# The order of sixteen products in a half block: high and low parts in turn, or eight and eight

## The chip, the cores and the metric

The kernel runs on one core of a Trainium2 chip. Its engines work in parallel, each on its own list of instructions in order: TensorE (PE, matrix products; its weight loads are listed as PEld), VectorE (DVE), ScalarE (ACT), GpSimd (POOL) and SyncE (SP, which here only issues DMAs). The metric is the device time of one execution in microseconds; the profile shows one execution, instruction by instruction.

## The reference

One encoder block works on 256 tokens of 2048 channels, all in float32. In short:

```python
proj = h @ w_in[l]                                   # 2048 -> q, k, v, r, af, ab, u (6144), gates (4096)
y_gla = _gla_branch(q, k, v, r, af, ab, ...)         # gated linear attention, both directions
y_hy = _hyena_branch(hy_u, ...)                      # short convolution, then two long ones by FFT
merged = g[:, :, 0, :] * (y_gla @ w_gla_o[l]) + g[:, :, 1, :] * (y_hy @ w_hy_o[l])
h = _layernorm(DEEPNORM_ALPHA * h + merged @ w_out[l], ln1_g[l], ln1_b[l])
ff = jnp.square(jax.nn.relu(h @ w_ff1[l])) @ w_ff2[l]  # 2048 -> 8192 -> 2048
h = _layernorm(DEEPNORM_ALPHA * h + ff, ln2_g[l], ln2_b[l])
```

Nearly all of the arithmetic is in the large products with the weight matrices.

## The kernel before, in words

**Three products for one.** The large products are made in the type float32r. A float32 weight w is split into a high part (whi, rounded to float32r by ACT, line 81) and a low part (wlo = w - whi, by DVE, line 82); the activations are split in the same way and lie side by side, high and low. The kernel adds up high x high, high x low and low x high.

**Weight blocks.** The weights come from device memory as blocks of 128 x 2048 float32 (1 MB each), in the order of their use. `fetch` (line 89) issues the DMA of a block on SP's queue into a tile `raw` (3 buffers) and splits it in two halves of 1024 columns, each with a tile `whi` and a tile `wlo` (3 buffers each). A half therefore holds eight 128 x 128 weight tiles, one for each of eight slices `kt` of the 2048 input channels. `next_block` (line 129) fetches one block more and hands out the oldest, so that two blocks are on their way while one is in use.

**Two ways to use a block.** In a channel pair (`channel_pair`, line 133) the weights are the stationary operand and the activations move. It makes 256 output channels for all 256 tokens, from two blocks, and for each block it takes an accumulator of 512 columns in PSUM: columns 0 to 255 collect high x high and low x high, columns 256 to 511 collect high x low. For each `kt` there are two products: line 143, weight high part, which streams 512 columns (activation high and low), and line 144, weight low part, which streams 256 columns (activation high) and adds into the first 256 columns of the accumulator. So a block takes 32 products, 16 in each half. Behind them ACT copies the second half of the accumulator (line 146) and DVE adds the first half to it (line 147). The channel pairs make q, k, the gates g1 and g2, the hyena inputs (uv, ux, uz), the output projections go and ho, and the first MLP product f (four quarters f0 to f3 of eight pairs each): 96 pairs, 192 blocks, 384 halves. A first block for the gate ranks (pa, lines 370 to 374) has the same loop. In a token group (`token_group`, line 166) the activations are stationary and the weights move, always 512 columns wide (lines 162 to 164): r, v, wo and the second MLP product w. The last column group of wo and of w (lines 790 to 792) is 256 wide.

**One special case.** The first block of f0 runs with `by_tile`: it makes the products for the first 128 tokens, then for the second 128, so that it can begin while the second half of the layer norm is still under way (the transposes ht, line 826).

**Side work.** Between blocks `pump` (line 116) adds smaller jobs that were put off with `later`: the hyena filters (ha, hb, Ca, Sa, Cb, Sb), the gates, scores and outputs of the four attention heads (z, s, o, yt), and the hyena's transforms (Zp, yp, vt, x1t, yT). They use PSUM buffers of their own.

**What sets the order.** The program is written in the order above, and an automatic scheduler then orders the instructions of every engine by a time line that it simulates; where the side work falls between the products is its decision. On the chip every engine follows its list and waits on semaphores.

The lines that the change and the prediction touch: 81 and 82 (split), 96 (DMA of a block), 143 and 144 (channel pair products), 146 and 147 (their sum), 162 to 164 (token groups), 346 (filters, DVE), 373 and 374 (first block), 541 (yt), 675 and 716 (hyena output to device memory and back), 776 and 826 (layer norm and transposes).

Of the kernel before, what the change touches and what calls it, by code (L numbers as in the profile page):

```python
# [16 lines left out]
P = 128  # L17
# [3 lines left out]
KT = D // P  # L21
# [19 lines left out]
def block_kernel(  # L41
# [24 lines left out]
    MM = nc.tensor.matmul  # L66
# [7 lines left out]
    def psum_main(name):  # L74
        return mmp.tile([P, 512], F32, tag="mm", name=name)
# [40 lines left out]
    def pump():  # L116
        clock[0] += 1
        due = sorted((e for e in side if e[0] <= clock[0]), key=lambda e: e[:2])
        for e in due:
            side.remove(e)  # L120
        for e in due:
            e[2]()
# [6 lines left out]
    def next_block():  # L129
        fetch()  # L130
        return queue.popleft()

    def channel_pair(act, name, dst=None, scale=1.0, by_tile=False):
        if dst is None:
            dst = base.tile([P, 2, L], F32, tag="sum", name=f"{name}_s")
        for c in range(2):
            ps = psum_main(f"{name}_{c}").rearrange("p (a b) -> p a b", a=2)
            parts = next_block()
            for ts in ((slice(0, P), slice(P, L)) if by_tile and c == 0 else (slice(0, L),)):
                for kt in range(KT):  # L140
                    hi, lo = parts[kt // 8]
                    js = slice(kt % 8 * P, (kt % 8 + 1) * P)
                    MM(ps[:, :, ts], hi[:, js], act[:, kt, :, ts], start=(kt == 0), stop=False)  # L143
                    MM(ps[:, 0, ts], lo[:, js], act[:, kt, 0, ts], start=False, stop=(kt == KT - 1))  # L144
            low = base.tile([P, L], F32, tag="low", name=f"{name}_l{c}")
            nc.scalar.activation(low, ps[:, 1], AF.Copy, scale=scale)
            nc.vector.scalar_tensor_tensor(dst[:, c], ps[:, 0], scale, low, op0=ALU.mult, op1=ALU.add)
            pump()
        return dst
# [40 lines left out]
    def act_tile(pool, tag, name):  # L190
        return pool.tile([P, KT, 2, L], F32R, tag=tag, name=name)
# [12 lines left out]
    xT = act_tile(base, "xT", "xT")  # L204
# [162 lines left out]
    pa = psum_main("pa").rearrange("p (a b) -> p a b", a=2)  # L367
    fetch()
    parts = next_block()
    for kt in range(KT):  # L370
        hi, lo = parts[kt // 8]
        js = slice(kt % 8 * P, (kt % 8 + 1) * P)
        MM(pa, hi[:, js], xT[:, kt], start=(kt == 0), stop=False)
        MM(pa[:, 0], lo[:, js], xT[:, kt, 0], start=False, stop=(kt == KT - 1))
    nc.scalar.copy(a_low, pa[:, 1])
    nc.vector.tensor_tensor(a_sum[:, 0], pa[:, 0], a_low, op=ALU.add)
    nc.scalar.copy(as_sb, a_sum[:, 0])
# [5 lines left out]
    for dst, nm, sc in ((q_sb, "q", 1.0 / 16.0), (k_sb, "k", 1.0)):  # L383
        for c2 in range(4):
            channel_pair(xT, f"{nm}{c2}", dst[:, 2 * c2:2 * c2 + 2, :], sc)
# [182 lines left out]
    for c2 in range(8):  # L568
        channel_pair(xT, f"g1_{c2}", m_pair(c2))
# [111 lines left out]
    def gla_o_pair():  # L681
        c2 = go_done[0]
        go_done[0] += 1
        ps = channel_pair(yT, f"go{c2}")
        mp = m_pair(c2)
        nc.vector.tensor_tensor(mp, mp, ps, op=ALU.mult)

    go_after = [0, 0, 1, 1, 1, 1, 1, 3]
    for c in range(NCH):
        ps = channel_pair(xT, f"uv{c}")  # L690
# [4 lines left out]
        ps = channel_pair(xT, f"ux{c}")  # L695
# [5 lines left out]
        ps = channel_pair(xT, f"uz{c}")  # L701
# [7 lines left out]
    for c2 in range(8):  # L709
        ps = channel_pair(xT, f"g2_{c2}")  # L710
# [8 lines left out]
    for c2 in range(8):  # L719
        ps = channel_pair(yhT, f"ho{c2}")  # L720
# [22 lines left out]
    def resident(slots):  # L743
        parts = []
        for hi, lo in slots:
            n = fetched[0]
            fetched[0] = n + 1
            raw = wp.tile([P, D], F32, tag="raw", bufs=3, name=f"raw{n}")
            nc.sync.dma_start(raw, wblk[n])
            for h in range(2):  # L750
                cs = slice(h * 1024, (h + 1) * 1024)
                split_hi_lo(hi[:, cs], lo[:, cs], raw[:, cs])
            parts.append([(hi[:, 0:1024], lo[:, 0:1024]), (hi[:, 1024:], lo[:, 1024:])])
        return parts

    def halves(pool, tag, name):
        t = pool.tile([P, 4, D], F32R, tag=tag, name=name)
        return [(t[:, 0], t[:, 1]), (t[:, 2], t[:, 3])]
# [49 lines left out]
    parts = resident([x0] + halves(ep, "f", "wr1"))  # L808
# [67 lines left out]
    parts = resident(halves(ep, "f", "wr2") + halves(ep, "hT", "wr3"))  # L876
# [137 lines left out]
```

## Time and profile before

| | |
|---|---|
| median of 3 runs | 1891.8 us (1891.52 to 1891.81) |
| profiled execution, its own time | 1891.83 us |
| its span | 1890.0 us |
| granted TensorE clock, mean | 0.994 |
| PE busy | 1860.4 us, 10060 matmuls |
| weight loads (PEld) busy | 1599.7 us |
| DVE busy | 1313.6 us |
| ACT busy | 949.5 us |
| read from device memory | 356.66 MB |

A busy time adds up the stretches in which an engine had an instruction under way. Matmuls are pipelined, so that the duration of one is longer than its share of the stream; the distance from one start to the next is what a matmul costs in a stream. In a row of the timeline the columns are the start and the duration in us, the engine, the line, the operation, output and inputs, the sizes of the stationary tile and of the moving one, and the number of instructions. "L144 ... 128x256" streams 256 columns.

### The profile page before, as it was taken

To read this page: it belongs to the slowest core of one execution; us is meant where nothing else is said; L and a number is where in the kernel's file an instruction comes from. 1 tells how busy PE (TensorE), PEld (TensorE's weight loads), DVE (VectorE), ACT (ScalarE), POOL (GpSimd) and SP (SyncE) were. 2 spreads that over 40 slices of the span, in tenths; PEclk is the share of its full clock that TensorE was granted. 3 is DMA by queue.
4 is the path that set the end of the run, shared out by engine and by line. 5 is a ranking of instruction groups with operands and counts; after the bars stand their busy time and mean duration, and the time that the engine had idled before them with its cause. 6 is when DMAs were issued, how large, how long until landed. Compare 5 with 4: busy or idle time off the path is not lost.

```text
span 1890.0 us, 25333 instructions
## 1 busy us (share of the span) xinstructions
PE 1860.4 (98%) x10060; PEld 1599.7 (85%) x10060; DVE 1313.6 (70%) x1702; ACT 949.5 (50%) x1286; POOL 38.3 (2%) x60
## 2 busy tenths in 40 slices
PE   8999999999999999999999998999999999999996
PEld 7887888888888888888888888888888888888886
DVE  6787968875789888888556567666555555555556
ACT  5555556674555555555544444444434443444343
POOL 0000000000000000000000001000000000000001
PEclk9999999999999999999999999999999999999998
DMA  7667764445555555565655764555555555545552
GB/s 289 231 225 251 265 228 161 140 142 204 195 195 199 199 194 189 197 223 191 212 197 183 285 216 153 188 193 186 196 186 198 180 199 187 192 180 199 191 189 110
DMA packets 60583, 375.09 MB, mean 198 GB/s; under 512 B 7216, under 2 KB 10928, under 8 KB 20912
## 3 DMA queue, kind: packets, MB, share of 16 engines
q1 hardware_dynamic: 46512, 324.03, 47.4%
q0 software_dynamic: 5888, 29.36, 4.2%
q10 hardware_dynamic: 8064, 20.07, 3.0%
q8 instruction: 79, 1.29, 0.3%
q14 instruction: 40, 0.33, 0.0%
HBM read 356.66 MB, written 16.78 MB: 198 GB/s over the span
## 4 chain that ended last, share of the span: by engine, by line
PE 93%; DVE 4%; ACT 1%; DMA 1%; issue 1%; ACTq 0%; DVEq 0%; SPq 0%
PE f L143 13%; PE f L144 6%; PE g L143 6%; PE w L163 6%; PE w L164 6%; PE w L162 6%; PE go L143 3%; PE ux L143 3%; PE uz L143 3%; PE uv L143 3%; PE g L144 3%; PE ho L143 3%; PE ho L144 2%; PE uv L144 2%; PE ux L144 2%; PE go L144 2%
## 5 line engine op out<-in xcount | busy, mean ns | idle before, releaser
L82 DVE TENSOR_TENSOR wlo<-raw,whi 128x1024 fp32r<-128x1024 f32 x596 | 728.3, 1223 | 488.2 <-ACT whi L81 487.3
L81 ACT CAST whi<-raw 128x1024 fp32r<-128x1024 f32 x596 | 627.0, 1053 | 772.6 <-PE w L164 186.8
L143 PE MATMUL f<-hT,whi 128*128 128x512 f32 (+1 forms) x1040 | 361.7, 394 | 0.0
L144 PE MATMUL f<-hT,wlo 128*128 128x256 f32 (+1 forms) x1040 | 290.0, 279 | 0.0
L143 PEld LDWEIGHTS f<-hT,whi 128*128 128x128 f32 x1040 | 195.6, 188 | 44.3
L144 PEld LDWEIGHTS f<-hT,wlo 128*128 128x128 f32 x1040 | 197.1, 190 | 0.1
L163 PE MATMUL w<-wlo,f 128*128 128x512 f32 x480 | 186.8, 389 | 0.0
L164 PE MATMUL w<-whi,f 128*128 128x512 f32 x480 | 186.8, 389 | 0.0
L143 PE MATMUL g<-xT,whi 128*128 128x512 f32 x512 | 178.6, 393 | 0.0
L162 PE MATMUL w<-whi,f 128*128 128x512 f32 x480 | 168.0, 389 | 0.0
L144 PE MATMUL g<-xT,wlo 128*128 128x256 f32 x512 | 143.5, 281 | 0.0
L143 PEld LDWEIGHTS g<-xT,whi 128*128 128x128 f32 x512 | 95.7, 187 | 21.1
L162 PEld LDWEIGHTS w<-whi,f 128*128 128x128 f32 x480 | 90.0, 188 | 18.8
L164 PEld LDWEIGHTS w<-whi,f 128*128 128x128 f32 x480 | 90.1, 188 | 18.7
L163 PEld LDWEIGHTS w<-wlo,f 128*128 128x128 f32 x480 | 90.1, 188 | 18.5
L144 PEld LDWEIGHTS g<-xT,wlo 128*128 128x128 f32 x512 | 96.7, 189 | 0.5 <-DVE wlo L82 0.2
L143 PE MATMUL uz<-xT,whi 128*128 128x512 f32 x256 | 91.9, 398 | 0.0
L143 PE MATMUL ux<-xT,whi 128*128 128x512 f32 x256 | 91.7, 398 | 0.0
L143 PE MATMUL go<-yg,whi 128*128 128x512 f32 x256 | 91.1, 397 | 0.0
L143 PE MATMUL uv<-xT,whi 128*128 128x512 f32 x256 | 90.5, 395 | 0.0
L143 PE MATMUL ho<-yh,whi 128*128 128x512 f32 x256 | 88.8, 391 | 0.0
L144 PE MATMUL ux<-xT,wlo 128*128 128x256 f32 x256 | 72.0, 281 | 0.0
(329 smaller groups left out, 3336.7 us busy)
## 6 DMA issues: line engine op xcount, KB each, us to landing
raw<-wblk SPq DMA_DIRECT2D x303, 1024.0 KB, 4.8
Td<-T POOLq DMA_DIRECT2D x16, 768.0 KB, 4.1
Tl<-Td POOLq DMA_DIRECT2D x16, 768.0 KB, 4.5
w<-w4s ACTq DMA_DIRECT2D x16, 512.0 KB, 4.6
zr<-ln_rows ACTq DMA_DIRECT2D x4, 1024.0 KB, 10.9
raw<-wblk SPq DMA_DIRECT2D x4, 512.0 KB, 6.7
xr<-xt SPq DMA_DIRECT2D x4, 512.0 KB, 6.5
dec<-decay_in ACTq DMA_DIRECT2D x8, 256.0 KB, 3.1
```

Of the source, the lines that this page charges most:

```text
L81: nc.scalar.copy(hi, src)
L82: nc.vector.tensor_tensor(lo, src, hi.bitcast(F32), op=ALU.subtract)
L143: MM(ps[:, :, ts], hi[:, js], act[:, kt, :, ts], start=(kt == 0), stop=False)
L144: MM(ps[:, 0, ts], lo[:, js], act[:, kt, 0, ts], start=False, stop=(kt == KT - 1))
L162: MM(pss[tb], sh, wh, start=(kt == 0), stop=False)
L163: MM(pss[tb], sh, wl, start=False, stop=False)
L164: MM(pss[tb], sl, wh, start=False, stop=(kt == KT - 1))
```

## The change

In each half block the products with `kt` from 0 to 7 (or 8 to 15) were issued in turn: high, low, high, low. Now the eight products on the high part come first and the eight on the low part behind them. The same happens in the loop of the first block (pa). Number, operands and results of the products are the same; only their order differs, and the first product of a block still starts the accumulator and its last one still ends it. The scheduler orders the rest anew.

```diff
             ps = psum_main(f"{name}_{c}").rearrange("p (a b) -> p a b", a=2)
             parts = next_block()
             for ts in ((slice(0, P), slice(P, L)) if by_tile and c == 0 else (slice(0, L),)):
-                for kt in range(KT):
-                    hi, lo = parts[kt // 8]
-                    js = slice(kt % 8 * P, (kt % 8 + 1) * P)
-                    MM(ps[:, :, ts], hi[:, js], act[:, kt, :, ts], start=(kt == 0), stop=False)
-                    MM(ps[:, 0, ts], lo[:, js], act[:, kt, 0, ts], start=False, stop=(kt == KT - 1))
+                for h in range(2):
+                    hi, lo = parts[h]
+                    kts = [(kt, slice(kt % 8 * P, (kt % 8 + 1) * P)) for kt in range(8 * h, 8 * h + 8)]
+                    for kt, js in kts:
+                        MM(ps[:, :, ts], hi[:, js], act[:, kt, :, ts], start=(kt == 0), stop=False)
+                    for kt, js in kts:
+                        MM(ps[:, 0, ts], lo[:, js], act[:, kt, 0, ts], start=False, stop=(kt == KT - 1))
...
     parts = next_block()
-    for kt in range(KT):
-        hi, lo = parts[kt // 8]
-        js = slice(kt % 8 * P, (kt % 8 + 1) * P)
-        MM(pa, hi[:, js], xT[:, kt], start=(kt == 0), stop=False)
-        MM(pa[:, 0], lo[:, js], xT[:, kt, 0], start=False, stop=(kt == KT - 1))
+    for h in range(2):
+        hi, lo = parts[h]
+        kts = [(kt, slice(kt % 8 * P, (kt % 8 + 1) * P)) for kt in range(8 * h, 8 * h + 8)]
+        for kt, js in kts:
+            MM(pa, hi[:, js], xT[:, kt], start=(kt == 0), stop=False)
+        for kt, js in kts:
+            MM(pa[:, 0], lo[:, js], xT[:, kt, 0], start=False, stop=(kt == KT - 1))
```

## The prediction

> **What bounds the kernel now.** I read the page first: the busy times and the chain of work that ended last.
>
> ```profile
> span 1890.0 us, 25333 instructions
> PE 1860.4 (98%) x10060; PEld 1599.7 (85%) x10060; DVE 1313.6 (70%) x1702; ACT 949.5 (50%) x1286; POOL 38.3 (2%) x60
> PE 93%; DVE 4%; ACT 1%; DMA 1%; issue 1%; ACTq 0%; DVEq 0%; SPq 0%
> L143 PE MATMUL f<-hT,whi 128*128 128x512 f32 (+1 forms) x1040 | 361.7, 394 | 0.0
> L144 PE MATMUL f<-hT,wlo 128*128 128x256 f32 (+1 forms) x1040 | 290.0, 279 | 0.0
> ```
>
> PE sets the time: it is busy 98% of the span and carries 93% of the chain. The two lines that the change reorders (L143 the high part, 512 columns; L144 the low part, 256 columns) show no idle time before them. Their means (394 and 279 ns) are latencies of overlapping matmuls, so I priced them by the distance from one start to the next, in the timeline of PE. Next, who PE waits for:
>
> ```profile
> PE ht L826 <- DVE zr L776: 5.3, 3, 3.0
> PE pa L373 <- DVE xT L82: 3.9, 1, 3.9
> PE v L163 <- DVE wlo L82: 1.4, 2, 0.9
> PE yt L541 <- DVE y L534: 1.3, 1, 1.3
> PE Cb L226 <- DVE T L346: 0.7, 1, 0.7
> PE v L163 <- DVE rq_t L184: 0.7, 1, 0.7
> ```
>
> Columns: total us, times, longest. None of these is a product of a channel pair waiting for a weight half, so giving wlo more time buys nothing there. What is left is the rate at which PE streams. A stretch of ho:
>
> ```profile
> 1000.16 0.39 PE L143 MATMUL ho<-yh,whi 128*128 128x512 f32 x1
> 1000.39 0.28 PE L144 MATMUL ho<-yh,wlo 128*128 128x256 f32 x1
> 1000.51 0.39 PE L143 MATMUL ho<-yh,whi 128*128 128x512 f32 x1
> ...
> 1004.32 0.39 PE L143 MATMUL ho<-yh,whi 128*128 128x512 f32 x1
> ```
>
> Twelve pairs in 4.16 us: 346.7 ns a pair, 230 ns after the 512-wide and 117 ns after the 256-wide one. The same code in the third quarter of f is slower:
>
> ```profile
> 1500.26 0.40 PE L143 MATMUL f<-hT,whi 128*128 128x512 f32 x1
> 1500.61 0.40 PE L143 MATMUL f<-hT,whi 128*128 128x512 f32 x1
> ...
> 1501.32 0.40 PE L143 MATMUL f<-hT,whi 128*128 128x512 f32 x1
> ```
>
> Three pairs in 1.06 us: 353.3 ns a pair, and it stays so for all of f2 and f3, with no wait in it. So the alternating stream has two rates, and a stretch keeps the one that it has. Streams of one width:
>
> ```profile
> 1844.90 0.40 PE L163 MATMUL w<-wlo,f 128*128 128x512 f32 x1
> ...
> 1846.06 0.39 PE L163 MATMUL w<-wlo,f 128*128 128x512 f32 x1
> ```
> ```profile
> 1853.38 0.39 PE L164 MATMUL w<-whi,f 128*128 128x512 f32 x1
> 1853.61 0.28 PE L790 MATMUL w<-wr,f 128*128 128x256 f32 x1
> 1853.72 0.28 PE L791 MATMUL w<-wr,f 128*128 128x256 f32 x1
> 1853.84 0.28 PE L792 MATMUL w<-wr,f 128*128 128x256 f32 x1
> ```
>
> Long runs of 512-wide matmuls settle at 226.7 ns, long runs of 256-wide ones at 120 ns, each with its own weight load. The first fence stands just behind two 256-wide matmuls: its five steps take 1.16 us where settled ones take 1.133. The second is the other switch.
>
> **The change, part by part.**
>
> *The rate of a settled half.* Instruction counts and operands stay; 192 blocks of channel pairs (and pa) have two halves each, 384 halves in all. Before, eight fast pairs: 8 x 346.7 = 2773 ns. After, from the settled rows: 8 x 226.7 + 8 x 120 = 2773 ns. No gain and no loss: only the two phase effects below are left.
>
> *The slow phase goes.* I took the distance from start to start of every matmul of a channel pair and subtracted the settled price (226.7 or 120 ns), leaving out single steps over 40 ns, which are waits and transposes. The remainder is 3.2 us in f, 3.9 us in uv, ux, uz and go together, 0.8 us in q and k, 0.6 us in g, 0.0 in ho: 8.5 us. f alone checks it: 512 pairs of f2 and f3 by 6.6 ns are 3.4 us. Runs of one width leave that phase: behind the slow f2, the first 512-wide steps of w are 233, 236, 228, 232, 231 and then 227 ns. After five matmuls it has settled, and the new groups are eight long. So -8.5 us.
>
> *Switching costs come in.* From settled 512 to 256 the steps are 114, 119, then 120 ns: 7 ns gained (second fence). From 256 to 512 the first five steps are 3 to 9 ns too long; the cases of the trace sum to 25 to 28 ns, and the last 256-wide step ahead of them is 1 to 3 ns short. Net 15 to 19 ns for a half, and I take 17.5: 384 x 17.5 ns = +6.7 us (5.8 to 7.3). Bounds: nothing, if the groups settle at once as in the alternating rows, up to 384 x 28 = 10.8 us if the 7 ns are not won.
>
> *Side work between the products.* 124 times in the trace a channel pair's product is followed by a matmul of another kind. Where that lands inside a group it starts another settling, up to 20 ns each: 0 to 2.5 us, taken as half, +1.2.
>
> *Weight halves and buffers.* whi is released seven short matmuls (0.84 us) earlier in each half, wlo at the same place, and the first wlo of a half is needed 7 x 0.227 = 1.6 us later. The cast L81 can start earlier and DVE's L82 waits less for it, but PE does not wait for either in these stages. The copy L146 waits, as before, for the block's last low product, so nothing is freed earlier in PSUM. Price 0; the cover is the two blocks fetched ahead.
>
> *The start.* pa's fifth high product comes 4 x 0.21 us (half clock) sooner than now, at about 12.1 us; its xT group is finished at 11.67. The ninth comes at 15.55 as today (its group: 14.5), the thirteenth at 16.5, and the last group is done at 15.77. No wait; 0.
>
> *Order elsewhere.* The order of the changed kernel shows the groups as written, SP's queue unmoved, and on POOL one load of yr put ahead of one store of yd. yr and the split of yh end at 917 us and ho begins at 976, so 59 us cover it. What does move is side work: counted in PE work, the filter products stand 4 to 9 us later in k and r, the first gates 5 us and later heads' scores 2.7 us later in v, the hyena steps 2 to 3 us later. Queued behind a late side product on PE is the main stream, so each is a possible wait; equally, inputs that now come 0.7 to 1.3 us late (Cb, v, yt above) have more time. For yt the trade can be counted: 38 products stood between its last o and it, 6.6 us, and it waited 1.3; now about 7.2 us stand there, but ACT's copy L146 (0.37 us) has entered the chain. It nets 0.2 us. The waits in r, v and g1 sum to 4.3 us; they can vanish or double, and I take 0 between. The waits of ht hang on a DVE order that is the same in both kernels, so 0.
>
> Sum: -8.5 + 6.7 + 1.2 = -0.6 us. The profiled execution took 1891.83 us (span 1890.0 and 1.83 around it), level with the median 1891.8. **Forecast: 1891.2 us.**
>
> One rule weighed against these rows. The Trainium skill, page "TensorE: Matmul & The Clock Gate", section "Back-to-back issue gap", gives an isolated gap of N/2.4 + 2.5 ns, that is 215.8 and 109.2 ns here, whatever stood before. The rows say 226.7 and 120, and show steps that depend on what stood before. By the rule alone the sum is 0 and the time 1891.8.
>
> **The rivals.**
>
> A, the settling costs nothing: groups of eight settle at once, as the fast alternation does with a switch at every step. For it: 230 + 117 equals 226.7 + 120. Against it: every switch to 512 behind a run of 256 in the trace costs. Then only the slow phase goes: 1891.8 - 8.5 = 1883.3 us.
>
> B, slower, by waits of PE for side work in r, v and g1. DVE is busy all 7 of the 7 us around 353, where PE waits 1.1 us for a wlo behind head 2's rows; if the shifted gates meet more wlo splits there, that wait repeats for each head. For it: DVE is that stage's limit. Against it: the shift gives inputs more time too. With the 4.3 us of waits doubled: 1891.2 + 4.3 = 1895.5; it decides from there up.
>
> C, weight loads bind. A load's record lasts 188 ns, and eight short matmuls in a row offer 120 ns each: 3072 x 68 ns = 209 us, 2100 us. Against it: L790 to L792 load for every 256-wide matmul and run at 120. The Trainium skill's section "LDWEIGHTS (loading the stationary operand)" of the same page gives 128/1.2 = 107 ns, which would fit under such a matmul; the 120 ns steps agree.
>
> That the change is not made is excluded by the order.
>
> **How the numbers follow.** Forecast 0.62, A 0.14 (with part of the settling cost it ends between), B 0.22, C 0.01, others 0.01. 0.2% is 3.8 us, about what a measurement of this kernel can tell. Faster by more needs A: 0.15. Slower needs B or C: 0.22. Same: 0.63. Range: the settling bounds (-7 to +4) matter less than B's waits upward; leaving out most of A below and the tail of B above gives 1886.5 to 1897. The forecast's own range is 1888.2 to 1895.
>
> **What would show it.** In f2 and f3 of the changed kernel, a half should take 2790 ns (16 products) against 2827 now, and in ho 2790 against 2773: f2 and f3 gain, ho, g2 and f0 lose. Within a half: steps of about 233, 235, 228, 232, 231, 227, 227, then 114, 119, 120. Steps that stay above 227 to the eighth, or above 120 among the short ones, refute the settling price; ho unchanged speaks for A. PE's waits should still be the six above within 2 us; new lines "v <- wlo" or "Cb <- T" over 4 us in sum are B. A busy weight load between short products is C. I am wrong if the groups hold a third rate, or a wait moves with the side work.

## The result and the profile after

The changed kernel takes 1888.74 us (median of 20 runs, 1887.83 to 1889.88), the kernel before 1891.86 us in the same job (20 runs, 1889.44 to 1897.27). The ratio is 0.9981 [0.9974, 0.9987]. That is 3.1 us less by the medians: inside the range, faster beyond the interval, and just short of the 0.2% (3.8 us) that the prediction had set as the bound of "same". Besides the median the spread moved: the runs of before lie within 8 us, those of the changed kernel within 2 us.

The profiled execution took 1888.03 us against 1891.83. First the page of the changed kernel: span, busy times, chain, and the two reordered lines (143 and 144 are now 144 and 146).

```profile
span 1886.3 us, 25333 instructions
PE 1858.3 (99%) x10060; PEld 1602.4 (85%) x10060; DVE 1312.3 (70%) x1702; ACT 954.8 (51%) x1286; POOL 38.3 (2%) x60
PE 96%; DVE 2%; ACT 1%; DMA 0%; issue 0%; ACTq 0%; SPq 0%; DVEq 0%
L144 PE MATMUL f<-hT,whi 128*128 128x512 f32 (+1 forms) x1040 | 259.3, 391 | 0.0
L146 PE MATMUL f<-hT,wlo 128*128 128x256 f32 (+1 forms) x1040 | 144.7, 282 | 0.0
```

PE still sets the time; its share of the chain grew from 93 to 96%, DVE's fell from 4 to 2%. The busy times of the two lines fell (361.7 to 259.3, 290.0 to 144.7 us), but that is only bookkeeping: a long and a short matmul under way at once no longer count twice. The means hardly moved (394 to 391, 279 to 282 ns). Next, who PE waits for in the changed kernel; the columns are total us, times, longest:

```profile
PE ht L830 <- DVE zr L780: 5.1, 3, 3.3
PE pa L376 <- DVE xT L82: 3.3, 1, 3.3
PE warm L222 <- DVE ones_sb L225: 1.5, 1, 1.5
PE yt L545 <- DVE y L538: 1.0, 1, 1.0
PE v L165 <- DVE wlo L82: 0.9, 1, 0.9
PE v L165 <- DVE rq_t L186: 0.7, 1, 0.7
PE g L144 <- DVE vl L82: 0.6, 1, 0.6
PE ht L830 <- DVE hT L82: 0.2, 1, 0.2
```

The wait of Cb (0.7 us) is gone, those of v, yt and pa are shorter, and there is one new wait, of g for the split of v (0.6 us). Last, the timeline of PE in the third quarter of f and in ho. Eight matmuls of a kind now stand in one row; columns are start and duration in us.

```profile
1479.81 1.11 PE L146 MATMUL f<-hT,wlo 128*128 128x256 f32 x8
1480.76 2.00 PE L144 MATMUL f<-hT,whi 128*128 128x512 f32 x8
1482.60 1.12 PE L146 MATMUL f<-hT,wlo 128*128 128x256 f32 x8
```
```profile
1005.38 1.11 PE L146 MATMUL ho<-yh,wlo 128*128 128x256 f32 x8
1006.33 2.00 PE L144 MATMUL ho<-yh,whi 128*128 128x512 f32 x8
1008.17 1.12 PE L146 MATMUL ho<-yh,wlo 128*128 128x256 f32 x8
```

From one group of low products to the next passes one half: 2.79 us in both stages. Before, it was eight pairs of 353.3 ns = 2.83 us in f2 and f3, and eight of 346.7 = 2.77 us in ho. The steps from start to start from 1479.81 on, in ns, worked out of the trace (one number for each product, the time to the next one):

```
low  113 119 120 120 120 120 120 120   high 234 236 228 232 231 227 227 226   low 114 119 120 120 120 120 120 120
```

**Where the time went.** As in the prediction I subtract the settled price (226.7 or 120 ns) from every step. Steps off by up to 40 ns are summed as "rate"; larger ones are waits, the transposes and the stretches at half clock. A step is counted in the stage of the product that opens it, so a wait stands with the product ahead of it. The settled price of all 10060 matmuls is the same in both kernels, so the two sums hold the difference of the two profiled executions (3.8 us) to within 0.1 us:

| us over the settled price | before | after |
|---|---|---|
| rate, f0 / f1 / f2 / f3 | -0.18 / 0.00 / 1.69 / 1.69 | 0.53 / 0.64 / 0.61 / 0.61 |
| rate, uv + ux + uz + go | 4.11 | 2.70 |
| rate, g1 + g2 + k + q | 1.55 | 1.94 |
| rate, ho | 0.00 | 0.64 |
| **rate, all channel pairs** | **8.85** | **7.68** |
| waits in r | 0.99 | 0.00 |
| waits in v | 3.04 | 2.36 |
| waits in g1 | 1.69 | 2.42 |
| waits of side work, with the start | 30.50 | 28.88 |
| **waits and the rest, all** | **45.21** | **42.59** |

The rate gave 1.2 us and the waits 2.6 us. The predicted trade took place; in these two executions more came from where the prediction had put nothing.

### The profile page after: what moved, and what is told of

Its sections match the earlier page's. It is cut to its first block, busy times and chain, and to the rows that moved or that the text cites. A ratio compares the mean times of both kernels' runs of the same rounds, so it can differ in the third digit from the quotient of the medians.

```text
span 1886.3 us, 25333 instructions
## 1 busy us (share of the span) xinstructions
PE 1858.3 (99%) x10060; PEld 1602.4 (85%) x10060; DVE 1312.3 (70%) x1702; ACT 954.8 (51%) x1286; POOL 38.3 (2%) x60
## 4 chain that ended last, share of the span: by engine, by line
PE 96%; DVE 2%; ACT 1%; DMA 0%; issue 0%; ACTq 0%; SPq 0%; DVEq 0%
PE f L144 12%; PE f L146 6%; PE g L144 6%; PE w L164 6%; PE w L166 6%; PE w L165 6%; PE ux L144 3%; PE uz L144 3%; PE uv L144 3%; PE go L144 3%; PE ho L144 3%; PE g L146 3%; PE ux L146 2%; PE uv L146 2%; PE go L146 2%; PE ho L146 2%
## 5 line engine op out<-in xcount | busy, mean ns | idle before, releaser
L144 PE MATMUL f<-hT,whi 128*128 128x512 f32 (+1 forms) x1040 | 259.3, 391 | 0.0
L146 PEld LDWEIGHTS f<-hT,wlo 128*128 128x128 f32 x1040 | 141.5, 190 | 9.8
L146 PE MATMUL f<-hT,wlo 128*128 128x256 f32 (+1 forms) x1040 | 144.7, 282 | 0.0
L144 PE MATMUL g<-xT,whi 128*128 128x512 f32 x512 | 129.5, 393 | 0.6 <-DVE vl L82 0.6
L146 PEld LDWEIGHTS g<-xT,wlo 128*128 128x128 f32 x512 | 70.1, 190 | 5.0
L146 PE MATMUL g<-xT,wlo 128*128 128x256 f32 x512 | 72.3, 282 | 0.0
L144 PE MATMUL ux<-xT,whi 128*128 128x512 f32 x256 | 66.0, 395 | 0.0
L144 PE MATMUL uz<-xT,whi 128*128 128x512 f32 x256 | 65.6, 394 | 0.0
L144 PE MATMUL go<-yg,whi 128*128 128x512 f32 x256 | 65.0, 393 | 0.0
L144 PEld LDWEIGHTS ho<-yh,whi 128*128 128x128 f32 x256 | 46.0, 189 | 8.2
```

## The experiments

Two questions: is the cost of a group really that of its switches, and is the slow rate of the alternating stream a fixed property of a stage or a state that it falls into? Later came a third: where the part that isn't rate comes from. All kernels with other orders share one edit, which makes the order of a block's 32 products a list:

```diff
+def STEPS(group):
+    """(low part?, kt) of a block's 32 products, in order."""
+    if group == "mirror":
+        return ([(0, k) for k in range(8)] + [(1, k) for k in range(16)] + [(0, k) for k in range(8, 16)])
+    out = []
+    for k0 in range(0, KT, group):
+        for low in range(2):
+            out += [(low, k) for k in range(k0, k0 + group)]
+    return out
```

Group 1 is the kernel before, group 8 the change. The first four kernels ran once each; the kernel before took 1894.15 us beside them.

### The kernel before, profiled again

No edit.

> The kernel before, unchanged, to see whether its two rates are a matter of chance. Phase theory: the rate that a stretch of alternating products has is set by the last disturbance, so another execution can have it elsewhere; where the settled price is exceeded it is by about 6.7 ns a pair (353.3 against 346.7), and the sum of this excess over all channel pairs, 8.5 us in the first profile, differs from execution to execution (0 to 3072 x 6.7 = 20 us) and takes the time with it. Fixed theory: the rate belongs to the code and its addresses; f2 and f3 are slow again, f0, f1 and ho fast, and the sum is 8.5 us within 1.

It took 1897.15 us, and its rate sum is 12.1 us instead of 8.85. The difference is f0 (1.38 us) and f1 (1.70 us): both had run at the fast rate in the first profile. The timeline of PE, first of the profile before, then of this one, in the same place of f1:

```profile
1190.04 0.39 PE L143 MATMUL f<-hT,whi 128*128 128x512 f32 x1
1190.27 0.28 PE L144 MATMUL f<-hT,wlo 128*128 128x256 f32 x1
...
1193.51 0.39 PE L143 MATMUL f<-hT,whi 128*128 128x512 f32 x1
```
```profile
1189.98 0.40 PE L143 MATMUL f<-hT,whi 128*128 128x512 f32 x1
1190.22 0.28 PE L144 MATMUL f<-hT,wlo 128*128 128x256 f32 x1
...
1193.51 0.40 PE L143 MATMUL f<-hT,whi 128*128 128x512 f32 x1
```

Ten pairs take 3.47 us in the one and 3.53 us in the other. Same kernel, same instructions, another rate: the slow rate is a state. The remaining 2.2 us of this execution are waits (47.4 against 45.2).

### Groups of eight in f alone

```diff
-            r = channel_pair(hT, f"f{qi}_{c2}", by_tile=(qi == 0 and c2 == 0))
+            r = channel_pair(hT, f"f{qi}_{c2}", by_tile=(qi == 0 and c2 == 0), group=8)
```

> Only the channel pairs of f have their products in groups of eight; all other pairs alternate as before. f waits for nobody. Phase theory: the 128 halves of f cost 18 to 20 ns each over the settled price, 2.4 us in sum, whatever f had before (3.2 us in the first profile), so the time goes down by what f's excess was, less 2.4: about 1 us, with all other stages as before. Rival, that the gain of the change comes from the waits for side work alone: f's sum does not matter, and the time is that of before within 0.5 us.

1889.92 us. The rate sums of f are 0.54, 0.64, 0.61 and 0.61 us, 2.40 in all, as in the changed kernel; every other stage has that of the kernel before. So the settling cost in f follows the order within its blocks, whatever the order of the other stages: 2.40 us over 128 halves are 18.8 ns a half. One thing was not expected: the wait of Cb in r was gone, though PE's list ahead of f is that of the kernel before, product for product.

### Groups of other lengths

```diff
-GROUP = 1
+GROUP = 8
-        ps = channel_pair(yhT, f"ho{c2}")
+        ps = channel_pair(yhT, f"ho{c2}", group='mirror')
-            r = channel_pair(hT, f"f{qi}_{c2}", by_tile=(qi == 0 and c2 == 0))
+            r = channel_pair(hT, f"f{qi}_{c2}", by_tile=(qi == 0 and c2 == 0), group=(4, 2, "mirror", 16)[qi])
```

> Groups of eight everywhere, but f0 with groups of four, f1 with groups of two, f2 with the second half mirrored (eight high, sixteen low, eight high, so that one switch in each direction is left for a block), f3 with groups of sixteen (all high products of a block, then all low ones), ho mirrored like f2. Settling theory (a run of 512-wide products behind 256-wide ones loses about 27 ns over its first five steps, the way back wins 7): the sum over the settled price is, by quarters of 16 blocks, 64 x 15 ns = 1.0 us in f0, 128 x 9 ns = 1.1 us in f1, 16 x 19 ns = 0.3 us in f2, f3 and ho, against 0.6 us with groups of eight. Rival, that a group has a rate of its own whatever its length: 0.6 us in every quarter and in ho.

1888.69 us. The timeline of PE in f0 (groups of four), f1 (of two) and f2 (mirrored: 16 of a kind in a row):

```profile
1189.64 1.09 PE L161 MATMUL f<-hT,whi 128*128 128x512 f32 x4
1190.57 0.64 PE L159 MATMUL f<-hT,wlo 128*128 128x256 f32 x4
1191.04 1.09 PE L161 MATMUL f<-hT,whi 128*128 128x512 f32 x4
```
```profile
1265.35 0.63 PE L161 MATMUL f<-hT,whi 128*128 128x512 f32 x2
1265.82 0.39 PE L159 MATMUL f<-hT,wlo 128*128 128x256 f32 x2
1266.05 0.62 PE L161 MATMUL f<-hT,whi 128*128 128x512 f32 x2
```
```profile
1480.10 3.82 PE L161 MATMUL f<-hT,whi 128*128 128x512 f32 x16
1483.75 2.08 PE L159 MATMUL f<-hT,wlo 128*128 128x256 f32 x16
1485.66 1.55 PE L161 MATMUL f<-hT,whi 128*128 128x512 f32 x6
```

| | switches to 512 in a quarter | rate sum, us | ns each |
|---|---|---|---|
| f0, groups of 4 | 64 | 0.87 | 14 |
| f1, groups of 2 | 128 | 0.43 | 3 |
| groups of 8 (changed kernel, f2) | 32 | 0.61 | 19 |
| f2, mirrored | 16 | 0.32 | 20 |
| f3, groups of 16 | 16 | 0.29 | 18 |
| ho, mirrored | 16 | 0.35 | 22 |

For runs of 8 and 16 the cost follows the number of switches, 18 to 22 ns each. For shorter groups it does not: those of two cost 0.43 us where I had expected 1.1. Two cycles of it take 234, 236, 115, 113 and 232, 231, 114, 119 ns, 697 ns a cycle where settled steps would take 693: the long steps still cost 4 to 9 ns each, but every short step there gains 1 to 7 ns.

### All sixteen high products, then all sixteen low ones

```diff
-GROUP = 1
+GROUP = 16
```

> Groups of sixteen in all channel pairs and in pa: all high products of a block, then all low ones. Settling theory: 192 switches to 512 columns in place of 384, so the excess of the channel pairs falls from 7.7 us (groups of eight) to about 4.5 us with the part of the side work, and the time from 1888.7 to about 1885.5 us. Rival, that groups held longer starve the splits (the first low half is released 16 products later, and each has three buffers only): PE waits for wlo or whi of several us in q, k, u and go, and the time is at or above 1889 us.

1887.53 us, with a rate sum of 4.36 us. Half the switches, and 3.3 us less than with groups of eight. The waits (45.3 us) are 2.7 us above those of the changed kernel, though: 2.2 of it in pa, where this execution had half clock from 11.1 to 17.9 us, and 0.7 in v. The wait of yt is 1.7 us instead of 1.0.

### The changed kernel, its mirror and the groups of sixteen, timed

The changed kernel as it is; `GROUP = 'mirror'` (8 high, 16 low, 8 high) and `GROUP = 16`. The kernel before took 1893.74 us in this job (25 runs, 1889.21 to 1897.22).

> The changed kernel once more, as a base for the two below. Phase theory: no group keeps a slow phase, so the excess of its channel pairs over the settled price is 7.7 us again (within 0.3), f0 to f3 about 0.6 us each, and its runs lie within about 2 us of each other, while those of the kernel before spread by 5 us or more. Time 1888.7 us, ratio 0.998. Rival, that the changed kernel has two rates too: another sum, and a spread like that of the kernel before.

> In every block eight high, sixteen low, eight high products, so that the next block's first eight join the last eight of this one. Switches are halved as with groups of sixteen, but a half's high part is still released with its half. Settling theory: excess of the channel pairs 4.4 us in place of 7.7, time 3 us under that of the changed kernel, 1885.5 us. Rival, that waits for weight halves decide: the low part of the second half is now needed 8 x 0.227 = 1.8 us earlier, so PE waits for wlo in q, k, u and go, and the time is that of the changed kernel or above it.

> Groups of sixteen again, timed. Settling theory: its one look had the excess of the channel pairs at 4.4 us, as reckoned, but a time only 1.2 us under that of the changed kernel, with 2.7 us more in waits and side work. If those were this execution's (the clock at the start, the filter rows), the median is 3 us under the changed kernel; if they belong to the order of the side work that the scheduler made for it, it stays at 1 to 1.5 us under.

| | median, us | runs | ratio to before | rate sum | waits and rest |
|---|---|---|---|---|---|
| groups of 8 | 1888.9 | 1887.84 to 1889.55 | 0.9975 [0.9966, 0.9984] | 7.71 | 42.8 |
| mirror | 1887.9 | 1886.13 to 1889.34 | 0.9973 [0.9963, 0.9983] | 4.78 | 44.3 |
| groups of 16 | 1886.48 | 1886.19 to 1887.08 | 0.9967 [0.9955, 0.9979] | 4.37 | 44.2 |

Groups of 16 are the fastest version: 2.4 us under groups of 8, no run of it above the lowest of those. Its waits, and then those of the mirror:

```profile
PE pa L392 <- DVE xT L96: 4.1, 3, 3.4
PE yt L559 <- DVE y L552: 1.7, 1, 1.7
PE v L180 <- DVE wlo L96: 1.4, 2, 0.9
```
```profile
PE yt L559 <- DVE y L552: 1.8, 1, 1.8
PE v L180 <- DVE wlo L96: 1.6, 2, 0.9
...
PE r L180 <- DVE wlo L96: 0.5, 1, 0.5
PE k L159 <- DVE wlo L96: 0.3, 1, 0.3
```

The mirror saves as much rate as the groups of 16, but by its median only 1.0 us of the 3 us that I had expected: r and k wait for low parts there, and in both versions yt waits 0.7 to 0.8 us more than in the changed kernel. So each order has waits of its own: against the changed kernel's second profile they took back 1.4 us (groups of 16) and 1.5 us (mirror) of the 3.3 and 2.9 us that the rate gained.

### A transpose to set the rate

The kernel before, with one 128 x 128 transpose on PE between a high and a low product in the third block of each quarter of f.

```diff
                     MM(ps[:, :, ts], hi[:, js], act[:, kt, :, ts], start=(kt == 0), stop=False)
+                    if extra is not None and c == 0 and kt == 4:
+                        pt = psum_side(f"{name}_x")
+                        nc.tensor.transpose(pt[:, 0:P], extra, ident)
                     MM(ps[:, 0, ts], lo[:, js], act[:, kt, 0, ts], start=False, stop=(kt == KT - 1))
```

> The kernel before, with one 128 x 128 transpose added in the third block of each quarter of f, between a high product and its low product (four in all, 0.35 us each with the gap behind it). In the first profile of the kernel before, a transpose with a low product behind it left the alternating stream in the fast phase 13 times of 14. Phase theory: f0 to f3 run at 346.7 ns a pair behind it, f's excess is under 0.5 us (3.2 us in the first profile, 6.5 us in the second), and the time is 2 to 5 us under that of the kernel before in spite of 1.4 us of added work. Rival, that the rate belongs to the buffers or the code: f2 and f3 stay at 353.3 ns, and the time rises by 1.4 us.

1894.9 us (1892.07 to 1902.5), ratio 1.0014 [1.0002, 1.0025]: not faster, and the expectation failed. Of the four quarters two were fast behind the transpose (f0, f2) and two slow (f1, f3). The timeline behind the transposes of f1 and of f2:

```profile
1277.74 0.28 PE L147 MATMUL f<-hT,wlo 128*128 128x256 f32 x1
1277.86 0.40 PE L143 MATMUL f<-hT,whi 128*128 128x512 f32 x1
...
1280.69 0.40 PE L143 MATMUL f<-hT,whi 128*128 128x512 f32 x1
```
```profile
1454.89 0.27 PE L146 MATMUL f_x<-ident,f 128*128 128x128 f32 x1
...
1455.12 0.40 PE L143 MATMUL f<-hT,whi 128*128 128x512 f32 x1
...
1457.90 0.39 PE L143 MATMUL f<-hT,whi 128*128 128x512 f32 x1
```

Eight pairs take 2.83 us in f1 and 2.78 in f2. f1 had been fast ahead of its transpose and was slow behind it; with f2 it was the other way. So a disturbance between the products sets the rate anew, but this disturbance doesn't decide which of the two follows. The steps behind the two transposes begin alike (201, 231, 118, 240 and 201, 233, 117, 235 ns) and then part. What decides it stays open.

### f alone and all but f, timed

Groups of eight in f alone, as above, and its opposite: `GROUP = 8`, with `group=1` in f. The kernel before took 1892.22 us in this job (27 runs, 1889.12 to 1896.23).

> Groups of eight in f alone, timed. Phase theory: f always costs 2.4 us over the settled price in place of 3.2 and 6.5 us in the two profiles of the kernel before, so the time falls by 1 to 4 us, about 2.5, and its spread shrinks. Rival, that the gain comes from the earlier stages (waits for side work): within 0.5 us of the kernel before.

> The counterpart: groups of eight in pa, q, k, g1, g2, uv, ux, uz, go and ho, while f alternates. Phase theory: the excess of these pairs goes from 5.6 to 5.3 us and the waits of r, v and g1 by about -1.4 us as in the two profiles of the changed kernel, so -1 to -2 us; f keeps its two rates and the spread stays wide, 4 us or more. With the run above it adds up to the changed kernel's -3 to -5 us. Rival: all of the -3 to -5 us lies here.

| | median, us | runs | ratio to before |
|---|---|---|---|
| groups of 8 in f alone | 1891.39 | 1888.49 to 1894.61 | 0.9995 [0.9987, 1.0004] |
| groups of 8 everywhere but in f | 1889.8 | 1889.0 to 1890.39 | 0.9983 [0.9974, 0.9992] |

The part in f can't be told from nothing (0.8 us by the medians, where I had expected about 2.5), and its runs still lie 6 us apart. The part outside f gives 2.4 us, against 3.1 us for the whole change in its job, and its runs lie within 1.4 us, where I had expected 1 to 2 us and a spread of 4 or more. Yet its rate sum, 8.57 us, is only 0.3 us below that of before: f2 and f3 are still slow. So what is gained there is not mainly rate. The waits of this kernel:

```profile
PE pa L392 <- DVE xT L96: 3.8, 1, 3.8
...
PE yt L559 <- DVE y L552: 1.0, 1, 1.0
PE v L180 <- DVE wlo L96: 0.9, 1, 0.9
PE v L180 <- DVE rq_t L201: 0.7, 1, 0.7
PE g L161 <- DVE vl L96: 0.6, 1, 0.6
```

They are those of the changed kernel: yt 1.0 instead of 1.3, v 0.9 instead of 1.4 for wlo, no Cb, and g 0.6 that is new. They come back in each of the four profiles with groups of eight around q, k, r, v and the gates (the changed kernel twice, this one, the one with other lengths). The waits of yt, v and g belong to the order; that of Cb was gone with groups in f alone too.

### Sixteen, and every second block the other way round

Groups of 16, but in every second block one high product first, then the 16 low ones, then the other 15 high ones, so that the runs of neighbouring blocks meet, but for that one product.

```diff
-                steps = STEPS(group)
+                steps = STEPS("low early" if c == 1 else group)
+    if group == "low early":
+        return [(0, 0)] + [(1, k) for k in range(KT)] + [(0, k) for k in range(1, KT)]
```

> Groups of sixteen, and every second block begins with one high product (which starts the accumulator), then its sixteen low ones, then its other fifteen high ones, so that low runs and high runs of neighbouring blocks meet. Settling theory: about one switch in each direction for a pair of blocks, the excess of the channel pairs falls from 4.4 to 2.5 to 3 us and the time by 1.5 us under groups of sixteen, to 1885 us. Rival, that waits decide: the low halves of every second block are needed 16 x 0.227 = 3.6 us sooner, PE waits for wlo in q, k, u and go, and the time is above that of groups of sixteen (1886.5 us).

1889.67 us (1888.13 to 1891.65), 0.9984 [0.9975, 0.9993]. The rate sum is 4.70 us where I had expected 2.5 to 3: the shared runs are broken up. In f2 and in ho, in the order of PE, such a block runs as 1 high, 8 low, 8 high, 8 low, 7 high: the scheduler put the products of its first half ahead of those of its second. Within the channel pairs that leaves 267 steps from a 256-wide to a 512-wide product, against 201 with groups of 16. The waits of the profiled execution, the slowest of its eleven, rose to 49.0 us: pa waits 5.3 us for xT, wo 0.8 for a low part, and yt 2.4, with a stretch at half clock behind it (410.5 to 413.9 us) that no other profile has there; g1, where both are counted, has 4.3 us. Against groups of 16 it saves no rate and loses by waits.

### The kernel before, a third time

> The kernel before a third time. Phase theory: its excess over the settled price in the channel pairs is somewhere between 4 and 15 us and not the same as in both earlier profiles (8.9 and 12.1 us), with a time that follows it, 1888 us plus about the excess less 5. Fixed theory: 8.9 us again.

1892.29 us, rate sum 8.79 us, quarter by quarter as in the first profile (f0 and f1 fast, f2 and f3 slow). Two of three profiles of this kernel agree, the third is 3.3 us higher: the two rates are no coin thrown anew in each stage, but not fixed either. The steps show where the difference comes in. f2 and f3 stand behind 512-wide products of w, and in all five profiles in which f alternates, the one with the transposes included, both begin with the same steps (227, 113, 233, 117, 241, 120 ns, to 1 ns) and are slow from there. f0 stands behind the transposes ht, whose waits differ, and f1 goes on at the rate that f0 had: these two are what changed between the executions.

**The wait in r, over all profiles.** Cb's wait for T stands behind a table that goes to device memory; DVE waits for that store (Td) before it writes T again. DVE's wait for it, in the profile before, in that with groups in f alone, in the changed kernel and in the mirror (total us, times, longest):

```profile
DVE T L344 <- DMA Td<-T: 15.5, 5, 5.0
```
```profile
DVE T L361 <- DMA Td<-T: 13.7, 5, 4.3
```
```profile
DVE T L346 <- DMA Td<-T: 12.2, 6, 3.4
```
```profile
DVE T L361 <- DMA Td<-T: 23.8, 9, 5.3
```

Where the longest of these waits is 4.9 us or more (the kernel before in three profiles, with the transposes, the mirror), PE waits in r or k for Cb or a low part, 1.0 to 1.4 us by the steps of r. Where it is 4.3 or less (the changed kernel twice, both with groups in f alone, all but f, the one with other lengths, groups of 16 twice, the last variant), it doesn't. The two go together in all fourteen profiles; the store was not varied by itself, so how much of its time is the order's and how much chance is left open.

## Why the prediction was right, and where it was not

**The rate of a settled half** and **switching costs come in.** Right in mechanism and size. The forecast had the steps 233, 235, 228, 232, 231, 227, 227 and then 114, 119, 120; the trace has 234, 236, 228, 232, 231, 227, 227, 226 and 114, 119, 120. A half of f costs 18.8 ns over the settled price, one of ho 20.0, where 17.5 was taken (15 to 19). With the side work's share, the forecast left the channel pairs 6.7 + 1.2 = 7.9 us of excess; the trace has 7.68. The groups of 16 confirm the count of switches: half as many, and 4.4 us. The two terms were off in opposite directions, though, and part of the hit is luck: at 18.8 to 20.0 ns, 384 halves are 7.2 to 7.7 us instead of 6.7, which leaves at most 0.5 us for the side work instead of 1.2 (an estimate from the rates of f and ho, which hold next to none).

**The slow phase goes.** -8.5 us was right for the profile shown (8.85 by the same count with all stages). But it is a property of one execution: the second profile of the same kernel would have given -12. What the change takes away by rate lies therefore between 1.1 and 4.4 us, depending on the execution of the kernel before (8.79, 8.85 or 12.11 us). That the stated -0.6 came within 0.6 us of it is luck in this respect: the profile read for the prediction was one in which f0 and f1 were fast.

**Side work between the products.** Within the 7.68 us; not measured by itself (the estimate above leaves it at most 0.5 us).

**Weight halves and buffers.** Right: no channel pair waits for a weight half behind the new order in the changed kernel. In the mirror one does (k, 0.3 us).

**The start.** Taken as 0, and 0.7 us shorter in the profile: q's first product starts at 17.78 us instead of 18.53. That is the clock. The columns here are window, then window length and PE busy, PEld, DVE, ACT, POOL with their instructions, the granted clock, the busy share of the DMA engines and GB/s; first the kernel before, its third profile, and the changed kernel:

```profile
0.00:17.00 17.00, 11.62 (x29) 7.59 (x30) 8.92 (x10) 8.61 (x8) 0.20 (x4) 0.80 0.85 311
```
```profile
0.00:17.00 17.00, 12.28 (x35) 7.69 (x36) 9.12 (x10) 8.60 (x8) 0.20 (x4) 0.90 0.88 318
```
```profile
0.00:17.00 17.00, 12.19 (x32) 7.16 (x33) 9.09 (x10) 8.61 (x8) 0.20 (x4) 0.90 0.86 316
```

The unchanged kernel also shows 0.90 in one of its profiles, where q starts at 17.47 us, so this part is not the change's. The "no wait" of the prediction didn't quite hold: with the earlier clock, pa's thirteenth high product was due before the last xT group was split (15.75 us), and the steps there are 0.27 us too long.

**Order elsewhere.** This is the term that was mis-sized. Taken as 0 between -4.3 and +4.3 us, it measured -2.6 us in the profile for all waits together, of which 0.7 is the clock of the start. By stage: r -1.0, v -0.7, g1 +0.7; the rest is spread over the filters and the other side work. In g1 the wait of yt is counted, 1.2 us instead of 1.4, and the steps between products of g1 rose by 1.0 us, 0.8 of it at the new wait for vl. For yt the prediction had counted +0.2, with ACT's copy in the chain: PE waits 1.0 us instead of 1.3. The size of the term was within the stated bounds; the middle was not.

How much of it is the change's can be read over several profiles. I leave out the start, ht and f, whose waits vary in both kernels, and sum the waits of the rest in two parts:

| us of waits | behind k, r and the filters | behind all other stages |
|---|---|---|
| alternating ahead of f (six profiles) | 1.5, 2.8, 2.3, 2.1, 0.3, 0.2 | 22.9 to 23.2 |
| groups of 8 ahead of f (four profiles) | 0.0 in each | 22.5 to 22.6 |

The right column comes back with the order, and the change is worth only 0.5 us there: 0.7 gained behind v and 0.4 in the attention heads (s and yt), against 0.7 lost in g1, and small changes elsewhere. The left column is the larger part, and it is not shown to be the change's: the two small values are those with groups in f alone, where PE's list there is that of the kernel before. The kernel with groups everywhere but in f fits this: -2.4 us by the medians, of which 0.3 is rate and 0.5 the right column; the remaining 1.6 us has the size of the left one.

**The rivals.** A (settling costs nothing, 1883.3 us) is refuted by the steps: ho lost 0.64 us, where A has 0. Its nearest sight is the groups of two, at 3 ns a switch. B (waits for side work, 1895.5) did come in its mechanism, with the other sign: of the two lines that were to show it, "Cb <- T" vanished (by the profiles above, not surely by the change) and "v <- wlo" fell from 1.4 to 0.9 us. The new wait g for vl is 0.6 us. C (weight loads bind, 2100): sixteen short products with a load each take 1.91 us in the mirrored f2 (1483.75 to 1485.66), 119.4 ns each. The formula of the Trainium skill, page "TensorE: Matmul & The Clock Gate", section "Back-to-back issue gap", for an isolated matmul (N/2.4 + 2.5 ns, which knows only the width) gave no change; in every profile here a step depends on its predecessors, 114 to 120 ns for the one width and 227 to 236 for the other.

**The numbers.** 1888.74 against 1891.2: 2.5 us off, of which 0.6 is rate (-1.2 instead of -0.6) and the rest waits and chance. "Same" at 0.63 stands by a narrow margin: the interval of the ratio reaches to 0.9974, past the bound, and in the second job the same two kernels gave 0.9975, 4.8 us by the medians, which is past it. The kernel before moved between the jobs (1891.86 and 1893.74 us), the changed one hardly (1888.74 and 1888.9).

**Open.** Why the runs of before lie 8 us apart and those of the changed kernel 2. It lies in the stages ahead of f: groups of eight there give 1.4 us of spread, groups in f alone leave 6. The state of the rate can give some us (3.3 between two profiles of f), but with the groups outside f alone, f itself still alternated and the spread was small. The waits behind k, r and the filters vary from 0.2 to 2.8 us where the order ahead of f is the old one and are absent with groups of eight there, so they are a candidate. No run here isolates it.

## What to carry to other kernels

Price a stream of matmuls by its steps from start to start, by width and by what stood before; then the cost of an order with runs of eight or more is a count of its switches, and longer runs of one width are the direction to go (here 16 and 16, 1886.48 us, better than both kernels). Shorter runs have to be measured: those of two cost 3 ns a switch. Where side work is placed by a scheduler, every reordering also draws a new set of small waits; here the difference in waits between two profiles was larger than the effect that was priced, and only 0.5 us of it is seen to come back with the order, so take them as a range around the sum, and let several runs, not one profile, decide. Compare the spread too: an order that looks equal in one profile can be steadier.

## What the runs showed of the hardware

- A stream that alternates 512 and 256 columns holds one of two rates, 346.7 or 353.3 ns a pair, the slow one for all of f2 and f3 (512 pairs, 181 us). Behind the 512-wide products of w it came in slow each time (ten starts of f2 and f3 in five profiles). f0 and f1 of the same kernel were seen in both, and a transpose between the products set it anew in either direction.
- Groups of two are nearly free (3 ns a switch), groups of eight or sixteen cost 18 to 22 ns a switch: the settling takes five long matmuls, and the short ones behind a switch give back 7 ns only once.
- Stretches at half clock, but for the one at the kernel's end, came in pieces of 3.4 us, one or two in a row: behind the start from 9.1 to 15.9 us in the kernel before and from 10.2 to 13.6 in the changed one, at ht from 1162.8 to 1169.6 and, in one profile with groups in f alone, only from 1164.2 to 1167.6. The Trainium skill, page "TensorE: Matmul & The Clock Gate", section "What's actually happening", gives the window by which the clock is decided as 3413 ns, running freely of the kernel's start; the traces agree, in the length and in that the place differs by execution. One such stretch more or less is 1.7 us of a busy engine (an estimate, half of 3.4), more than the 1.2 us gained by the rate here.
